# Weight-sum copies spread over the attention stage, the adding transfers begun after its middle, six of them tied to tiles of the out-projection's second half

## The chip, the cores and the metric

One core of one Trainium2 chip runs the whole program. The metric is device microseconds (us) of one launch, here the median of three runs. A core has a matmul engine (PE, with PEld for its weight loads), VectorE (DVE), ScalarE (ACT), GpSimd (POOL) and SyncE (SP). SP, ACT and POOL also issue DMAs; these run on 16 DMA engines that all issuers share. In the profile, q0 is the DMA queue that POOL feeds ("software_dynamic"), q1 the one that SP feeds and q10 the one that ACT feeds ("hardware_dynamic").

## The reference, cut to what matters

One encoder layer over 1024 tokens of width 1024, all float32. The projected tokens go to two groups of heads; both are concatenated, projected out and added to x; then comes an MLP with a squared ReLU.

```python
h = rms(x, norm1_g)
p = h @ w_in
mix_a = mlstm_group(...)             # 4 heads, chunkwise matrix memory, gated by sigmoid(o)
mix_b = diff_attention_group(...)    # 4 heads; two softmax maps each, subtracted; 128-query blocks
x = x + concat(mix_a, mix_b) @ w_out
u = square(relu(rms(x, norm2_g) @ w_ff1))
x = x + u @ w_ff2
```

## The kernel before

Every matmul of float32 data is made of three products of a high and a low part (`mm3`, and the same by hand in `product`, `coarse_step`, `fine_step`): an operand arrives "raw" by DMA, ACT writes its high part, and DVE or POOL subtracts that from the raw tile to get the low part.

The MLP's second product is done by two nested levels of a Strassen-Winograd scheme. It needs sums and differences of blocks of `w_ff2`. These are not made on an engine: a DMA copies one block to a scratch tensor in DRAM, and a second DMA adds another block to it in DRAM (`accum_op=add`). `s7`, `s6`, `s5` hold the sums of the coarse level (8 pieces of 512 KB each), `so[i, p]` those of the fine level (2 pieces each). In `coarse_sums` and `fine_sums`, "c7" is the copy into sum 7, "a7" the add to it, and so on. The copies of the first sums and all adds are issued by POOL: line 186 is the copy (`copy_in`), line 189 the add (`add_to`). They are first read some 90 us into the MLP or later.

Order of the work around the change. The attention stage runs from about 342 to 580 us. It is 32 items (a head and 128 queries each); their pieces, and those of other work, are pushed on a heap with a time in units of one item and are written out in order of that time, so that each engine gets its instructions in that order and then waits only for what its data need. In order of time:

- Item n: `att_logits` (PE `pl`, then DVE l.1442 with the bias `toe`), `att_exp` (ACT l.1448), `att_weights` (DVE l.1454 to l.1458), `att_across` (PE l.1465, ACT l.1469), `att_product` (PE `pav`, l.1477), ACT l.1482, a root on POOL (l.1486 and l.231) and DVE l.1491. Every fourth item loads the next head: `q` and `kk` by POOL (l.1412, l.1415), `toe` and `v` by SP (l.1418, l.1423).
- Times 0 to 12: the gate's units (`gate_unit`), which end in a write of `mx_dram` by POOL (l.1604).
- Time 15.2: `swap` gives the memory of the first stages to the out-projection's tiles and loads `mix` for its first half by POOL (`load_mix`, l.1515, four loads of 512 KB).
- Times 18.4 to 34: `first_half`, eight tiles of the out-projection for tokens 0 to 511. The raw weights of a tile come by SP (`split_ahead`, l.1552, tile `raw_wo`, two buffers); ACT makes the high part `hi_wo` (l.270, by the helper `act`), POOL the low part `lo_wo` (l.1559).
- From time 34.3: the second half, tokens 512 to 1023, eight tiles `n`: `h_part` (24 matmuls of 128x512), `h_room` (loads x), `h_add` (DVE l.1728), `h_square` (ACT l.1734, and a store of y on ACT's queue), `h_sum`. Here DVE makes `lo_wo`. Between them stand `row_norms(0)` (PE l.1522, DVE l.1524, POOL l.231, PE l.1529) and the first weights and inputs of the MLP (l.1798 and l.1801, loads at l.1817).

The copies and adds stand on the same heap with times of their own: the copies of "c7" from time -2.5 on, 0.8 apart, the last of the 16 copies at 12.2; the eight coarse adds from 5.6 to 13; the eight fine adds from 18 to 27. The order on the queue of POOL is thus that of these times. The later sums (c6 and a6, c3 and a3, c5 and a5) are issued in the MLP by another table, and are not touched.

Of the kernel before, what the change touches and what calls it, by code (L numbers as in the profile page):

```python
# [140 lines left out]
def hybrid_block_kernel(ctx: ExitStack, tc: tile.TileContext, xT, xR, w_v, w_k, w_c, w_va, w_qg, w_o, w_1, w_2, w_2q, vec, rel, outT):  # L141
    nc = tc.nc
# [27 lines left out]
    def w2_block(row, col):  # L170
        return w_2[2 * row + col]
# [19 lines left out]
    def chain(i, q):  # L191
        o = {p: so[i, p][q] for p in (5, 6, 7, 3)}
        x = {(rr, b): w2_fine(i, rr, b)[q] for rr in range(2) for b in range(2)}
        return {
            "c7": (copy_in, o[7], x[0, 0]), "c5": (copy_in, o[5], x[1, 1]), "a7": (add_to, o[7], x[1, 0]),
            "a5": (add_to, o[5], x[1, 0]), "c6": (copy_in, o[6], o[7]), "a6": (add_to, o[6], x[1, 1]),
            "c3": (copy_in, o[3], o[6]), "a3": (add_to, o[3], x[0, 1]),
        }

    def fine_sums(what, i):  # L200
        return [chain(i, q)[x] for x in what.split() for q in range(2)]

    def coarse_sums(what):
        return [{
            "c7": (copy_in, s7[j], w2_block(0, 0)[j]), "a7": (add_to, s7[j], w2_block(1, 0)[j]),
            "c6": (copy_in, s6[j], s7[j]), "a6": (add_to, s6[j], w2_block(1, 1)[j]),
            "c5": (copy_in, s5[j], w2_block(1, 0)[j]), "a5": (add_to, s5[j], w2_block(1, 1)[j]),
            "a3": (add_to, s6[j], w2_block(0, 1)[j]),
        }[what] for j in range(8)]

    def spread(first, each, transfers, put):
        for n, (f, *args) in enumerate(transfers):
            put((first + each * n, 10**6 + 100 + n, f, args))
# [10 lines left out]
    cst = const.tile([P, 32], F32, name="cst")  # L224
# [111 lines left out]
    with tc.tile_pool(reuse_waits="tile", name="ps0", bufs=1, space=PSUM) as ps0:  # L336
# [219 lines left out]
        for i in range(2):  # L556
            n, k = [f"n{2 * i}", f"n{2 * i + 1}"], [f"kr{2 * i}", f"kr{2 * i + 1}"]
# [109 lines left out]
        for i, slot in enumerate((0, 1, 2, 4)):  # L667
            y = i % 2
# [40 lines left out]
        for t in range(4):  # L709
            y = t % 2  # L710
# [59 lines left out]
    clock, table, made = [0.0], [], []  # L770

    def when(t, f, *args):
        heapq.heappush(table, (t + moved.get(len(made), 0.0), len(made), f, args))
        made.append(t)
# [744 lines left out]
    def row_norms(half):  # L1519
# [16 lines left out]
    A = dict(  # L1536
        G0=-0.05, G1=0.219, E0=0.984, E1=1.396, W=1.626, A0=2.667, A1=2.819, C0=2.714, C1=2.824, P=3.534, SQ=3.666,
        RS=3.676, ON=3.783, TU=4.131, TH=4.141, TL=4.177, LD=-2.901, LV=-1.095, PF=-4, PS=1.015, PE=0.388, PT=1.671,
        PB=1.957, PW=-3.566, PH=-2.613, PL=-1.973, PX=-0.258, SW=15.195, OF=18.423, OS=0.979, OE=0.323, OQ=0.587,
        OA=1.385, OW=-3.888, OH=-2.551, OL=-2.267, HF=34.3, HS=0.375, LM=33, HE=0.3, HQ=0.415, HA=0.425, HW=-1.4,  # L1540
        HH=-0.861, HL=-0.4, HX=-3.083, S2=35.3, N0=36.2, N1=36.9, XN=37.278, XD=0.78, XH=1.108, XL=1.118, WN=37.523,
        WD=0.8, WL=0.227, RE=35.494,
    )
    clock[0] = -99.0

    def split_ahead(tiles, src, lo_eng, t, pre, floor=-99.0):

        T = {}

        def room():  # L1550
            T[0] = tiles()
            nc.sync.dma_start(T[0][2][:, 0:1024], src)

        def hi():
            act(T[0][0][:, 0:1024], T[0][2][:, 0:1024], AF.Copy)

        def lo():
            h, l, raw = T[0]
            lo_eng.tensor_tensor(l[:, 0:1024], raw[:, 0:1024], h[:, 0:1024].bitcast(F32), op=ALU.subtract)

        floor = max(floor, A["SW"] + 0.01 if pre in "OH" else -99.0)
        when(max(t + A[pre + "W"], floor), room)
        when(max(t + A[pre + "H"], floor), hi)
        when(max(t + A[pre + "L"], floor), lo)
        return T

    def gate_pieces():

        w_at = [A["PF"] + 4 * h * A["PS"] for h in range(NH)]
        for h in range(NH):  # L1570
            T = gate_w[h] if h < 2 else split_ahead(lambda h=h: w_tiles(f"o{h}"), w_c[8 + h], nc.gpsimd, w_at[h], "P")
            for g in range(2):
                gate_unit(h, g, T, w_at[h] + 2 * g * A["PS"])
# [55 lines left out]
    def w_out(n, half=0):  # L1629
        raw = opool.tile([P, 1024], F32, tag="raw", name=f"raw_wo{half}{n}", bufs=2)  # L1630
        hi = opool.tile([P, 1024], F32R, tag="woh", name=f"hi_wo{half}{n}", bufs=3)
        return hi, opool.tile([P, 1024], F32R, tag="wol", name=f"lo_wo{half}{n}", bufs=3), raw
# [63 lines left out]
    def push(x):  # L1696
        heapq.heappush(table, x)

    def at_times(slots, transfers):
        for (f, *args), t in zip(transfers, slots):  # L1700
            push((t, 10**6 + 200 + len(table), f, args))

    spread(-2.5, 0.8, coarse_sums("c7") + fine_sums("c7 c5", 1), push)
    spread(9.2, 1.0, fine_sums("c7 c5", 2), push)
    at_times((5.6, 6.4, 7.5, 8.5, 10, 11, 12, 13), coarse_sums("a7"))
    at_times((18, 19, 20, 22, 23, 24, 26, 27), fine_sums("a7 a5", 1) + fine_sums("a7 a5", 2))
    gate_pieces()
    when(A["SW"], swap)
    first_half()
# [43 lines left out]
    def room_at(n):  # L1753
        return A["HF"] + u * ends[n - 3] + 0.01 if n > 2 else -99.0

    for n in range(KT):
        t = A["HF"] + u * parts_at[n][0][0]
        V = {"w": split_ahead(lambda n=n: w_out(n, 1), w_o[n], nc.vector, t, "H", room_at(n))}
        for p, first, end in parts_at[n]:
            when(A["HF"] + u * p, h_part, V, n, first, end)  # L1760
        t = A["HF"] + u * ends[n]
        when(max(t + A["HX"], A["S2"] + 0.02), h_room, n)
        when(t + A["HE"], h_add, V, n)
        when(t + A["HQ"], h_square, V, n)
        when(t + A["HA"], h_sum, V, n)

# [79 lines left out]
    for j in range(4):  # L1846
        t = A["XN"] + j * A["XD"]
# [3 lines left out]
        t = A["WN"] + j * A["WD"]  # L1851
# [19 lines left out]
    table = []  # L1871
# [36 lines left out]
    for c in range(N_FIRST):  # L1908
        when(max(2 * c - 1, 0), ops[1], c)
        ends_at[1, c] = max(2 * c, 1)  # L1910
        t = min(2 * c + 2, 2 * N_FIRST - 1)
        when(t, ops[2], c)
        ends_at[2, c] = t + 1
    t = 2 * N_FIRST
# [230 lines left out]
    step_at, t = [], T2  # L2145
# [230 lines left out]
                tt(o, o, banks[n][:, sl], op=add)  # L2376
                eng.dma_start(outT[n][:, HB + sl.start : HB + sl.stop], o)

    pace = cst[:, 25:26]

    def add_after(s, f, *args):
        nc.gpsimd.tensor_copy(pace, graw[s][:, 0, 0:1])
        f(*args)
# [5 lines left out]
    for s, (i, p, x) in enumerate(steps):  # L2389
        t, e = step_at[s], step_at[s + 1]  # L2390
# [29 lines left out]
        if not p and x == NJ - 1:  # L2420
            for n in range(4):
                f = t + 0.5 * (n + 1) + (-0.01 if i == 5 else 0.01)
# [12 lines left out]
    for k in range(2):  # L2435
# [5 lines left out]
        for m, (d, name, row, half) in enumerate(((r00, "ea", 0, 0), (r01, "eb", 0, 1), (zv, "ec", 1, 0), (zx, "ed", 1, 1))):  # L2441
            t = d0 + 1.2 + 1.6 * (2 * m + k)
# [95 lines left out]
```

## Time and profile before

| | before |
|---|---|
| three runs | 1233.06 us median (1230.11 to 1233.25) |
| the profiled execution, its own time | 1233.69 us |
| its span, first to last instruction | 1231.9 us |
| PE busy | 1212.0 us (98%) |
| PEld, DVE, ACT, POOL busy | 1035.4, 893.0, 693.3, 282.9 us |
| mean granted clock of PE | 0.996 |
| DMA | 290.47 MB, 236 GB/s over the span |
| POOL's adds in DRAM (l.189) | 32 of coarse, 24 of fine sums, each issue about 0.81 us on POOL |

The profiled execution's span lies 1.8 us under its own time; that time is 0.6 us over the median. PE is busy nearly all the time, so what it loses stands in a few idle gaps. A profile line of a wait reads: who waited, on what, for how long, how often, and the longest one. In the timeline, the bracket is the idle time of that engine just before the instruction and what ended it. A row of a window has the busy time of PE, PEld, DVE, ACT and POOL with counts, then the granted clock, the mean busy share of the 16 DMA engines and what they moved in GB/s.

### The profile page before, as it was taken

How to read it: one execution, taken by the hardware profiler on the slowest of the kernel's cores; microseconds unless marked ns; L12 is line 12 of the kernel's file. 1: busy time of each engine (PE TensorE's matmuls, PEld its weight loads, DVE VectorE, ACT ScalarE, POOL GpSimd, SP SyncE). 2: the span in 40 equal slices, each digit the busy share in tenths (PEclk: the TensorE clock that was granted, in tenths of full speed). 3: DMA queues.
4: the chain of work that ended last, by engine and by line, in shares of the span. 5: the costliest groups of instructions: out<-in, count | busy, mean ns of one | idle time of the engine just before them, and what ended most of it. 6: DMA issues, size and time to landing. Idle time of an engine off the chain costs nothing.

```text
span 1231.9 us, 18385 instructions
## 1 busy us (share of the span) xinstructions
PE 1212.0 (98%) x6781; PEld 1035.4 (84%) x6781; DVE 893.0 (72%) x1253; ACT 693.3 (56%) x1200; POOL 282.9 (23%) x339
## 2 busy tenths in 40 slices
PE   9999999999999979999999999999999999999998
PEld 7889888888878868888887878888888999989987
DVE  7885568983267776765879886666657878888865
ACT  7785457676356666564455544545446556465532
POOL 2135323652356655431000000010100000010100
PEclk9999999999999989999999999999999999999999
DMA  9972665344589998745544789999899889998977
GB/s 283 229 248 104 208 145 132 99 139 129 162 305 279 289 303 225 208 138 205 179 165 144 265 280 306 259 256 276 255 275 355 281 287 337 353 306 249 257 260 260
DMA packets 115406, 290.47 MB, mean 236 GB/s; under 512 B 11632, under 2 KB 24432, under 8 KB 114544
## 3 DMA queue, kind: packets, MB, share of 16 engines
q1 hardware_dynamic: 85076, 202.88, 48.2%
q0 software_dynamic: 18432, 65.05, 22.7%
q10 hardware_dynamic: 11808, 21.37, 4.7%
q8 instruction: 53, 0.87, 0.3%
q14 instruction: 37, 0.30, 0.1%
HBM read 229.91 MB, written 112.82 MB: 278 GB/s over the span
## 4 chain that ended last, share of the span: by engine, by line
PE 80%; DMA 9%; DVE 4%; ACT 3%; issue 2%; POOL 1%; SPq 0%; ACTq 0%; DVEq 0%; POOLq 0%
PE m L1885 6%; PE m L1887 6%; PE m L1886 6%; PE z L2269 5%; PE z L2268 5%; PE z L2267 5%; PE pav L1477 5%; PE pl L1437 4%; PE pva L1347 4%; PE z L2288 3%; PE z L2287 3%; PE z L2286 3%; PE pw L280 3%; PE pw L282 2%; PE pw L281 2%; PE pa L1465 2%
## 5 line engine op out<-in xcount | busy, mean ns | idle before, releaser
L1442 DVE CUSTOM_DVE_ANT_0 l<-pl,toe 128x1024 f32<-128x1024 f32 x64 | 76.3, 1221 | 15.9 <-PE pl L1437 14.4
L189 POOL DMA_DIRECT2D so<-in_w_2q_dram x24 | 20.2, 842 | 277.2 <-DMA so<-so 242.0
L1934 ACT ACTIVATE sq<-sq 128x512 f32<-128x512 f32 x48 | 30.3, 630 | 83.3 <-DVE sq L1973 65.0
L1448 ACT ACTIVATE l<-l,sm 128x1024 f32<-128x1024 f32 x64 | 73.1, 1148 | 0.5 <-DVE sm L1442 0.5
L1477 PEld LDWEIGHTS pav<-v,at 128*128 128x128 f32 x512 | 63.0, 195 | 3.4 <-issue 1.1
L1477 PE MATMUL pav<-v,at 128*128 128x128 f32 x512 | 64.1, 279 | 0.0
L189 POOL DMA_DIRECT2D s<-in_w_dram x32 | 26.7, 844 | 157.0 <-DMA s<-in_w_dram 94.6
L1437 PE MATMUL pl<-kk,q 64*128 64x512 f32 x384 | 56.0, 415 | 3.0 <-DVE sm L1442 3.0
L2269 PE MATMUL z<-weh,wa0l 128*128 128x512 f32 x144 | 56.3, 391 | 0.1
L2267 PE MATMUL z<-weh,wa0h 128*128 128x512 f32 x144 | 56.2, 390 | 0.0
L2268 PE MATMUL z<-wel,wa0h 128*128 128x512 f32 x144 | 56.2, 390 | 0.0
L280 PE MATMUL pj_c<-hhi,w_c 128*128 128x512 f32 x128 | 53.4, 417 | 0.0
L280 PE MATMUL pw<-mix,hi_wo 128*128 128x512 f32 x128 | 52.0, 406 | 0.0
L282 PE MATMUL pj_c<-hhi,w_c 128*128 128x512 f32 x128 | 50.2, 392 | 0.0
L282 PE MATMUL pw<-mix,lo_wo 128*128 128x512 f32 x128 | 50.0, 391 | 0.0
L281 PE MATMUL pj_c<-hlo,w_c 128*128 128x512 f32 x128 | 50.0, 390 | 0.0
L281 PE MATMUL pw<-mix,hi_wo 128*128 128x512 f32 x128 | 49.9, 390 | 0.0
L2288 PE MATMUL z<-zgh,zwl 128*128 128x256 f32 x168 | 47.6, 284 | 0.8 <-DVE zwl L1801 0.8
L1437 PEld LDWEIGHTS pl<-kk,q 64*128 64x128 f32 x384 | 35.1, 186 | 15.6 <-DVE sm L1442 4.6
L2286 PE MATMUL z<-zgh,zwh 128*128 128x256 f32 x168 | 47.6, 283 | 0.3 <-ACT zwh L1798 0.3
L2287 PE MATMUL z<-zgl,zwh 128*128 128x256 f32 x168 | 47.5, 283 | 0.0
L1458 DVE SCALAR_TENSOR_TENSOR l<-l,sm,l 128x1024 f32<-128x1024 f32 x32 | 42.8, 1337 | 1.1
(544 smaller groups left out, 4061.6 us busy)
## 6 DMA issues: line engine op xcount, KB each, us to landing
s<-in_w_dram POOLq DMA_DIRECT2D x40, 512.0 KB, 8.3
so<-in_w_2q_dram POOLq DMA_DIRECT2D x32, 512.0 KB, 8.5
g_dram<-gs SPq DMA_DIRECT2D x64, 256.0 KB, 5.8
zw<-s SPq DMA_DIRECT2D x32, 512.0 KB, 7.2
g<-g_dram SPq DMA_DIRECT2D x32, 512.0 KB, 8.6
wide<-g_dram SPq DMA_DIRECT2D x24, 512.0 KB, 8.5
zw<-so SPq DMA_DIRECT2D x24, 512.0 KB, 3.5
g_dram<-sq ACTq DMA_DIRECT2D x42, 256.0 KB, 4.2
```

The costliest lines, as they stand in the source:

```text
L280: nc.tensor.matmul(out, ahi, bhi, start=start, stop=False)
L281: nc.tensor.matmul(out, ahi, blo, start=False, stop=False)
L282: latest[0] = nc.tensor.matmul(out, alo, bhi, start=False, stop=stop).ins
L1437: nc.tensor.matmul(it.pl[x][:, sl], hd.q[r, i, qi * P : (qi + 1) * P], hd.kk[r, j, sl], start=n == 0, stop=n == 2)
L1442: nc.vector.tensor_tensor_reduce(lt, it.pl[m], hd.toe[:, off : off + S], 1.0, 3.0e38, ALU.add, ALU.min, it.sm[:, m : m + 1])
L1477: nc.tensor.matmul(it.pav[:, 0:P], at, it.head.v[:, c], start=c == 0, stop=c == NC - 1)
L2267: nc.tensor.matmul(p, wh, gh, start=go, stop=False, skip_group_check=True)
L2268: nc.tensor.matmul(p, wh, gl, start=False, stop=False, skip_group_check=True)
L2269: nc.tensor.matmul(p, wl, gh, start=False, stop=end, skip_group_check=True)
L2286: nc.tensor.matmul(o, wh[:, j, nn], gh[:, j], start=go, stop=False, skip_group_check=True)
L2287: nc.tensor.matmul(o, wh[:, j, nn], gl[:, j], start=False, stop=False, skip_group_check=True)
L2288: nc.tensor.matmul(o, wl[:, j, nn], gh[:, j], start=False, stop=end, skip_group_check=True)
```

## The change

The 16 first copies get a list of times of their own, from -2.5 to 21.2, where they had stood at -2.5 to 12.2: twelve of them up to 13.2, four at 18.2 to 21.2. The 16 first adds are taken as one list. Ten of them (the eight coarse ones, and the two that add to `so[1, 7]`) stand at 19.7 to 29.6, 1.1 apart. The other six are pushed right behind `h_add` of the tiles n = 1 to 6 of the second half, each by `add_with`: a copy of one column of that tile's sum to the scratch column `pace` on POOL, which has to wait for the tile, and then the add. `pace` is the column that `add_after` uses later for other adds; its definition only moves up. No transfer is added or taken away; six copies of 128x1 on POOL are new.

```diff
-    spread(-2.5, 0.8, coarse_sums("c7") + fine_sums("c7 c5", 1), push)
-    spread(9.2, 1.0, fine_sums("c7 c5", 2), push)
-    at_times((5.6, 6.4, 7.5, 8.5, 10, 11, 12, 13), coarse_sums("a7"))
-    at_times((18, 19, 20, 22, 23, 24, 26, 27), fine_sums("a7 a5", 1) + fine_sums("a7 a5", 2))
+    first_copies = coarse_sums("c7") + fine_sums("c7 c5", 1) + fine_sums("c7 c5", 2)
+    first_adds = coarse_sums("a7") + fine_sums("a7 a5", 1) + fine_sums("a7 a5", 2)
+    at_times((-2.5, -1.7, -0.9, -0.1, 1.2, 2.6, 4.2, 6.2, 7.6, 9.2, 11.2, 13.2, 18.2, 19.2, 20.2, 21.2), first_copies)
+    spread(19.7, 1.1, first_adds[:10], push)
+    pace = cst[:, 25:26]
+
+    def add_with(n, f, *args):
+        nc.gpsimd.tensor_copy(pace, y[1][n][:, 0:1])
+        f(*args)
+
     gate_pieces()
...
         when(t + A["HE"], h_add, V, n)
+        if 1 <= n < 7:
+            f, *args = first_adds[9 + n]
+            push((t + A["HE"] + 0.005, 10**6 + 200 + len(table), add_with, (n, f, *args)))
         when(t + A["HQ"], h_square, V, n)
```

The order of PE, ACT, DVE and SP stays as it was; only POOL's changes. Around `swap`, POOL had this before (s and so are the scratch tensors; `128x1024` marks an add, `16x8192` a copy; mx_dram, q, kk and mix as above; sm are the roots of the items):

```order
L189 DMA s_6_183<-in_w_dram 128x1024
L186 DMA so_1_210<-in_w_2q_dram 16x8192
L1456 TENSOR_SCALAR sm_4266<-sm_4266 128x1
L1486 TENSOR_TENSOR sm_4113<-sm_4113 128x1
L231 TENSOR_TENSOR sm_4113<-sm_4113,mhalf 128x1
L189 DMA s_7_184<-in_w_dram 128x1024
L1412 DMA q_4405<-q_dram_76 128x1024
L1415 DMA kk_4407<-k_dram_67 128x2x512
```

and has this now; the adds are gone, and one copy stands behind the loads of kk:

```order
L186 DMA so_0_201<-in_w_2q_dram 16x8192
L1456 TENSOR_SCALAR sm_4186<-sm_4186 128x1
L1486 TENSOR_TENSOR sm_4039<-sm_4039 128x1
L231 TENSOR_TENSOR sm_4039<-sm_4039,mhalf 128x1
L1456 TENSOR_SCALAR sm_4257<-sm_4257 128x1
L1486 TENSOR_TENSOR sm_4106<-sm_4106 128x1
L231 TENSOR_TENSOR sm_4106<-sm_4106,mhalf 128x1
L1412 DMA q_4392<-q_dram_76 128x1024
L1415 DMA kk_4394<-k_dram_67 128x2x512
L1415 DMA kk_4394<-k_dram_68 128x2x512
L186 DMA so_1_202<-in_w_2q_dram 16x8192
```

In the second half, POOL had after the items' last root only the two roots of the row norms (rc), and behind them adds of the MLP:

```order
L231 TENSOR_TENSOR sm_5707<-sm_5707,mhalf 128x1
L231 TENSOR_TENSOR rc_6064<-rc_6064,mhalf 128x4
L231 TENSOR_TENSOR rc_6322<-rc_6322,mhalf 128x4
L189 DMA so_0_203<-in_w_2q_dram 128x1024
L189 DMA so_1_204<-in_w_2q_dram 128x1024
```

and now has the six copies (of the tile y) and adds, one pair ahead of the first rc, five between the two:

```order
L231 TENSOR_TENSOR sm_5701<-sm_5701,mhalf 128x1
L1710 COPY cst<-y_0_5963 128x1
L189 DMA so_0_201<-in_w_2q_dram 128x1024
L231 TENSOR_TENSOR rc_6060<-rc_6060,mhalf 128x4
L1710 COPY cst<-y_1_5964 128x1
L189 DMA so_1_202<-in_w_2q_dram 128x1024
L1710 COPY cst<-y_1_5964 128x1
L189 DMA so_0_213<-in_w_2q_dram 128x1024
```

The four pairs that follow these in the list, up to the second rc, read alike.

More of the change, by code (lines that the diff above doesn't have):

```diff
@@ L2377, in finish @@
                 eng.dma_start(outT[n][:, HB + sl.start : HB + sl.stop], o)
-    pace = cst[:, 25:26]
     def add_after(s, f, *args):
```

## The prediction

> **What bounds the kernel now.** The page first. PE is busy for 98% of the span, so a change pays only where PE stands idle or cold. I then cut the span into stretches; in these columns (stretch, length, busy PE, PEld, DVE, ACT, POOL, clock, DMA share, GB/s) one place in the attention stage stands out:
>
> ```profile
> PE 1212.0 (98%) x6781; PEld 1035.4 (84%) x6781; DVE 893.0 (72%) x1253; ACT 693.3 (56%) x1200; POOL 282.9 (23%) x339
> 430.00:440.00 10.00, 9.36 (x73) 7.69 (x73) 9.57 (x17) 7.77 (x17) 6.21 (x13) 1.00 1.07 309
> 440.00:450.00 10.00, 8.51 (x63) 6.74 (x62) 6.16 (x11) 3.67 (x9) 1.69 (x2) 1.00 1.09 402
> 450.00:460.00 10.00, 5.62 (x34) 5.31 (x36) 6.63 (x11) 7.24 (x16) 7.33 (x9) 0.66 0.65 194
> 460.00:480.00 20.00, 20.00 (x135) 16.71 (x132) 14.47 (x26) 12.44 (x24) 10.30 (x13) 1.00 0.91 234
> ```
>
> From 430 to 460 PE loses 6.5 us, at a DMA share of 1.07 and 1.09, and the clock then falls to 0.66; from 460 on PE is full. Next the waits of 428 to 462, and the chain through it:
>
> ```profile
> ACT hi_wo L270 <- DMA raw_wo<-in_w_o_dram: 6.0, 1, 6.0
> 435.18 14.46 DMA raw_wo<-in_w_o_dram
> 450.63 1.24 ACT l L1448 x2
> ```
>
> The raw weights of the out-projection's first tile need 14.46 us. ACT stands at their high part, with two items' exponentials behind it, and for those wait DVE (l.1458) and, by the last bracket below, PE. The timeline gives the sizes:
>
> ```profile
> 449.67 1.06 ACT L270 ACTIVATE hi_wo<-raw_wo 128x1024 fp32r<-128x1024 f32 x1 [5.98 <-DMA raw_wo<-in_w_o_dram]
> 441.60 1.97 PE L1437 MATMUL pl<-kk,q 64*128 64x512 f32 x12
> 446.35 2.18 PE L1437 MATMUL pl<-kk,q 64*128 64x512 f32 x12
> 454.38 1.09 PE L1465 MATMUL pa<-ident,l 128*128 128x128 f32 x4 [5.85 <-DVE l L1458]
> 455.26 3.33 PE L1477 MATMUL pav<-v,at 128*128 128x128 f32 x16
> 458.95 1.66 PE L1437 MATMUL pl<-kk,q 64*128 64x512 f32 x12
> ```
>
> ACT was free at 443.69 (449.67 - 5.98). Two items' `pl` follow each other after 4.75 us (441.60 to 446.35); the next comes after 12.60. So the place costs 7.85 us: 5.85 of idling, the rest in matmuls run cold after it.
>
> Why was the tile late? The queues of 426 to 438 and then of 438 to 450 (the row of packets is the latter's), and landing times of `v` over the attention and of `raw_wo` at 460 to 535:
>
> ```profile
> q0 software_dynamic: 1007, 3.43, 103.1%
> q1 hardware_dynamic: 10, 0.03, 0.7%
> q<-q_dram POOLq DMA_DIRECT2D x1, 512.0 KB, 9.9
> DMA packets 2231, 4.79 MB, mean 399 GB/s; under 512 B 140, under 2 KB 1164, under 8 KB 2231
> q1 hardware_dynamic: 1490, 2.23, 52.7%
> q0 software_dynamic: 741, 2.56, 56.5%
> DMA to landing us min/median/max: 3.8/4.0/8.1
> DMA to landing us min/median/max: 3.4/5.0/6.5
> ```
>
> Until 438 POOL's queue alone fills all engines and works off a backlog (`q` lands after 9.9 us). SP's queue, which has `v` in small packets and then the tile, gets nearly nothing until then and about half afterwards.
>
> **The change, part by part.** *Price of a transfer.* Two adds nearly alone on q0 (520.2 to 534.5), then two copies with one store of mx_dram (362.5 to 372):
>
> ```profile
> so<-in_w_2q_dram POOLq DMA_DIRECT2D x2, 512.0 KB, 7.3
> q0 software_dynamic: 288, 1.05, 41.5%
> q0 software_dynamic: 214, 1.57, 42.6%
> ```
>
> 41.5% of 14.3 us is 5.9: some 3.0 us of all 16 engines per add. 42.6% of 9.5 is 4.05 for three: 1.35 per copy or store.
>
> *Adds and copies leave the time before the tile.* POOL's copies and adds of 512 KB in the last 32 us before it lie between the first two of these rows:
>
> ```profile
> 404.91 0.54 POOL L186 DMA_DIRECT2D so<-in_w_2q_dram  x1
> ...
> 427.04 0.86 POOL L189 DMA_DIRECT2D s<-in_w_dram  x1
> 434.76 0.37 SPq L1423 DMA_DIRECT2D v<-va_dram  x1
> 436.48 2.23 POOL L1515 DMA_DIRECT2D mix<-mx_dram  x4
> ```
>
> With three more adds and three more copies between them these are four adds and four copies, 4 x 3.0 + 4 x 1.35 = 17.4 us of engine time. The new order keeps three copies (times 9.2, 11.2, 13.2), 4.1 us. 13.3 us of transfer go from a stretch whose backlog was about 6 (9.9 for `q`, against 3.8 for `v` when nothing is ahead). The backlog should be gone by 427; what stays in front is q, kk, one copy and mx_dram.
>
> When does the tile land then? Its issue at 435.18 stays, since SP's order does. Early end: `v` 3.8 after 434.76, the tile 3.4 later, 442.0, before ACT comes at 443.69: no wait. Late end: all of v, two raw tiles, mx_dram and the four loads of mix, 8 x 0.524 = 4.19 MB, at 399 GB/s from 436.48, so 447.0: a wait of 3.3. I take 1.4, a little under the middle, because the tile is in front of half of these bytes. ACT still does the 1.06 of the high part within one item; between 0 and 1.06 of it reaches PE, I take 0.4. Gain: 7.85 - 1.4 - 0.4 = 6.05.
>
> The Trainium skill speaks against this: "DMA: Bandwidth & Descriptors", section "Queues, rings and completion order", says that a DMA engine takes turns between the queues that have work, a packet each. By that a backlog on POOL's queue costs SP's half of the engines, never all; the trace's 52.7% beside 56.5% agrees, and the 0.7% before 438 would be mostly SP having asked for nothing until 434.76. By this rule the gain would be the 2.55 of the first rival below, by the rows on the backlog 6.05.
>
> *The start of the attention* (to 404): one copy fewer between 342 and 351, adds gone. PE has no gap there that a DMA ends, so 0.
>
> *The middle, 455 to 530.* Before, three adds stood at times 18 to 20; now four copies and two adds stand at 18.2 to 21.2: 4 x 1.35 - 3.0 = 2.4 us more in about 24, on a share of 0.91. That fills the engines, but loads run far ahead:
>
> ```profile
> 466.48 0.37 SPq L1552 DMA_DIRECT2D raw_wo<-in_w_o_dram  x1
> 489.51 2.45 POOL L1559 TENSOR_TENSOR lo_wo<-raw_wo,hi_wo 128x1024 fp32r<-128x1024 f32 x1
> ```
>
> That is the fourth tile, loaded 23 us ahead of its low part; a landing of even 14.46 is hidden. 0. POOL's issues (0.54 to 0.9) move between the same kind of roots: 0. Without that cover each late tile would cost what the first did.
>
> *Six adds behind tiles 1 to 6 of the second half.* On POOL: six copies, which the same copy elsewhere (l.2382) prices at 0.2 to 1.1 us, and six issues of 0.8 to 0.9. The queue behind a waiting copy holds only the other pairs and the two rc roots; POOL idles 11.83 us ahead of the first of these, so the one pair in front fits: 0.
>
> ```profile
> L2382 POOL COPY cst<-g x8: 184/742/1118, 1093.1 to 1163.0; 128x1 f32<-128x1 f32 x8
> 591.91 1.40 POOL L231 TENSOR_TENSOR rc<-rc,mhalf 128x4 f32<-128x4 f32 x1 [11.83 <-DVE rc L1524]
> ```
>
> On the DMA engines: five of the adds, 15 us, go into 590 to 622, where 0.45 x 10 + 0.44 x 10 + 0.59 x 12 = 16 are taken:
>
> ```profile
> 590.00:600.00 10.00, 10.00 (x53) 8.53 (x52) 6.90 (x11) 3.64 (x6) 1.40 (x1) 1.00 0.45 164
> 600.00:610.00 10.00, 10.00 (x45) 8.27 (x45) 9.94 (x14) 6.20 (x8) 0.00 (x0) 1.00 0.44 152
> 610.00:622.00 12.00, 12.00 (x54) 9.95 (x53) 8.72 (x11) 4.40 (x6) 0.00 (x0) 1.00 0.59 188
> 602.26 0.38 SPq L1552 DMA_DIRECT2D raw_wo<-in_w_o_dram  x1
> 606.71 1.06 ACT L270 ACTIVATE hi_wo<-raw_wo 128x1024 fp32r<-128x1024 f32 x1 [0.96 <-DMA raw_wo<-in_w_o_dram]
> 609.70 1.22 DVE L1559 TENSOR_TENSOR lo_wo<-raw_wo,hi_wo 128x1024 fp32r<-128x1024 f32 x1
> 619.97 0.69 DVE L1728 TENSOR_TENSOR y<-pw,y 128x512 f32<-128x512 f32 x1 [2.52 <-PE pw L282]
> ```
>
> 31 of 32: just full. The last tile is the tightest. It lands by 606.7; high and low part take 1.06 + 1.22; PE ends it at 619.97, and its 24 matmuls (10 us per 45) take 5.4, so PE needs it at 614.5. Slack 5.5. In the middle, where adds were about all the time, such a tile landed after 6.5 at worst, 3.4 at best; 3.1 later is hidden. Lower bound 0 (the adds free nothing here); upper bound a landing of 14.46 instead of 4.4, 10.1 later, 4.6 lost. I take 0.4, near the row of the same kind of traffic.
>
> Sum: 6.05 - 0.4 = 5.65 us less. On the profiled execution's 1233.69 that is 1228.0; it lies 0.6 above the median, and on the median of 1233.06 it gives 1227.4.
>
> **The rivals.** *The tile stays late, 1230.5.* If not the backlog but sharing with the loads of mix holds it, only the start of SP's service moves, by at most 3 us (438 to 435). For it: after 438 SP's queue had its half, and more than half of the packets were small ones that take turns with mix's. Against it: with the backlog gone, `v` is through before mix begins. The tile then moves by 1 to 3; with 1.5 the wait stays at 4.5 and the gain is 7.85 - 4.5 - 0.4 - 0.4 = 2.55.
>
> *The second half takes it back, 1234.6.* The adds hold SP's tiles as the backlog did. The place is the last tile; it decides from a landing of 9.9 us on (4.4 + 5.5), and net from 6.05 us of loss. At 14.46 PE loses 4.6 there; the weights of the MLP's first products come behind it on the same queue, equally late, against a gap of 2.52 on DVE: 10.1 - 2.52 = 7.6 in all. 1233.06 - 6.05 + 7.6 = 1234.6. Against it: an add comes once per tile of 5.4 us and needs 3.0, where before 438 adds, copies and the attention's loads came together.
>
> **How the numbers follow.** A change under about 0.3%, 3.7 us, cannot be told from none. My forecast (1225 to 1229) has 0.70; the late tile 0.16 (0.13 within 0.3%); the second half 0.08 (0.05 within); the rest, all idle and cold time gone or something unseen, 0.06. Faster 0.77, same 0.18, slower 0.05. The low end is the whole 7.85 off the median, 1225.2, and 1.2 for where a median of three can lie among runs 3 us apart; the high end takes in the late tile and 1 us of the same.
>
> **What would show it.** Right: `hi_wo`'s wait of 5.98 under 3, `q` before it landing in about 5, `pl` no more than 8 us apart there, the clock of that stretch near 1, PE full at 584 to 622. Wrong: the wait over 4, or a new row of PE waiting for `hi_wo` or `lo_wo` in the second half.

## The result, and the profile after

| | before | after |
|---|---|---|
| median of the runs timed side by side | 1234.47 us (1230.11 to 1237.09) | 1226.59 us (1223.67 to 1231.93) |
| the profiled execution, its own time | 1233.69 us | 1227.73 us |
| its span | 1231.9 us | 1225.9 us |

The ratio of the times is 0.9939, with a 95% interval of 0.9925 to 0.9953: faster by 5.8 to 9.3 us, 7.88 between the medians of thirteen runs each. The two profiled executions, one of these runs each, differ by 5.96 us. The changed kernel's lines from l.1700 on stand 6 to 9 lower (`h_add` is l.1734, its copy to `pace` l.1710).

First the same stretches as before, in the same columns (stretch, length, PE, PEld, DVE, ACT, POOL, clock, DMA share, GB/s):

```profile
430.00:440.00 10.00, 9.36 (x74) 7.73 (x73) 9.57 (x17) 7.73 (x17) 6.17 (x13) 1.00 0.99 310
440.00:450.00 10.00, 9.81 (x76) 8.09 (x75) 8.41 (x18) 9.60 (x20) 6.69 (x8) 1.00 1.07 403
450.00:460.00 10.00, 9.77 (x69) 7.99 (x69) 8.09 (x16) 5.43 (x13) 6.84 (x11) 1.00 0.81 238
```

From 440 to 460 PE is busy for 19.58 of 20 us, where it was 14.13, and the clock stays at 1.00. From 440 to 450 the DMA engines are as full as they were (1.07 against 1.09); what the change relieved lies ahead of that. The timeline of the changed kernel at the place of the stall:

```profile
441.63 1.96 PE L1437 MATMUL pl<-kk,q 64*128 64x512 f32 x12
443.62 1.05 ACT L270 ACTIVATE hi_wo<-raw_wo 128x1024 fp32r<-128x1024 f32 x1
446.37 2.20 PE L1437 MATMUL pl<-kk,q 64*128 64x512 f32 x12
451.50 0.49 PE L1437 MATMUL pl<-kk,q 64*128 64x512 f32 x1
452.21 1.65 PE L1437 MATMUL pl<-kk,q 64*128 64x512 f32 x11 [0.23 <-DVE sm L1442]
453.79 0.50 PE L280 MATMUL pw<-mix,hi_wo 128*128 128x512 f32 x1
```

`hi_wo` has no bracket any more: the tile was there when ACT came. The two items' `pl` start at the same times as before (441.6 and 446.4), the third after 5.13 us instead of 12.60. The first matmul of the out-projection stands here at 453.79; before, it was this row:

```profile
460.55 0.50 PE L280 MATMUL pw<-mix,hi_wo 128*128 128x512 f32 x1
```

The queues of 426 to 438 in the changed kernel:

```profile
q0 software_dynamic: 874, 2.62, 71.3%
q1 hardware_dynamic: 476, 0.24, 7.0%
...
q<-q_dram POOLq DMA_DIRECT2D x1, 512.0 KB, 3.9
```

POOL's queue has 71.3% instead of 103.1%, SP's comes in before 438, and `q` lands after 3.9 us instead of 9.9. In the second half, where the six adds now are, the windows:

```profile
590.00:600.00 10.00, 10.00 (x46) 8.28 (x45) 9.86 (x14) 4.11 (x5) 3.36 (x3) 1.00 0.91 225
600.00:610.00 10.00, 10.00 (x46) 8.29 (x45) 8.29 (x10) 5.38 (x6) 4.07 (x4) 1.00 0.84 216
610.00:622.00 12.00, 12.00 (x63) 10.16 (x62) 7.81 (x12) 3.41 (x5) 4.34 (x3) 1.00 0.91 239
```

And from the timeline the last tile's load and its high part:

```profile
595.53 0.38 SPq L1552 DMA_DIRECT2D raw_wo<-in_w_o_dram  x1
602.93 1.06 ACT L270 ACTIVATE hi_wo<-raw_wo 128x1024 fp32r<-128x1024 f32 x1 [3.92 <-DMA raw_wo<-in_w_o_dram]
```

The engines' share, 0.44 to 0.59 before, is 0.84 to 0.91, the tile lands after 7.4 us instead of 4.4, ACT waits 3.92, and PE has no gap: the wait is hidden.

### The profile page after: what moved, and what is told of

Read it like the earlier page. It is cut to its first block, busy times and chain, and to the rows that moved or that the text cites. A ratio compares the mean times of both kernels' runs of the same rounds, so it can differ in the third digit from the quotient of the medians.

```text
span 1225.9 us, 18401 instructions
## 1 busy us (share of the span) xinstructions
PE 1211.5 (99%) x6781; PEld 1034.3 (84%) x6781; DVE 892.4 (73%) x1253; ACT 693.8 (57%) x1200; POOL 289.6 (24%) x345
## 4 chain that ended last, share of the span: by engine, by line
PE 83%; DVE 5%; DMA 5%; ACT 2%; issue 2%; POOL 1%; SPq 0%; ACTq 0%; DVEq 0%; POOLq 0%
PE m L1894 6%; PE m L1896 6%; PE m L1895 6%; PE z L2278 5%; PE z L2277 5%; PE z L2276 5%; PE pav L1477 4%; PE pva L1347 4%; PE pl L1437 3%; PE z L2297 3%; PE z L2296 3%; PE z L2295 3%; PE pvz L486 3%; PE pw L280 3%; PE pw L282 2%; PE pw L281 2%
## 5 line engine op out<-in xcount | busy, mean ns | idle before, releaser
L1347 PE MATMUL pva<-w_va,hhi 128*128 128x512 f32 x128 | 43.5, 403 | 0.0
```

Of the source, the lines that this page charges most:

```text
L1347: latest[0] = nc.tensor.matmul(p[:, j * HB : (j + 1) * HB], a, b, start=k == 0 and i == 0, stop=k == KT - 1 and i == 2).ins
```

## The experiments

Theory one, that of the prediction: the adds' backlog on POOL's queue held the first tile; what counts is how many us of transfers stand ahead of it. Its rival there: the tile shares the engines with the loads of `mix`, whatever stands ahead. Each run below was timed beside the kernel before (medians there 1233.1 to 1234.5); "wait" is ACT's idle time before the first tile's `hi_wo` in the one profiled execution. A difference between two rows whose intervals overlap is not shown.

| run | median, us | ratio to before, 95% | wait, us |
|---|---|---|---|
| the changed kernel | 1226.59 | 0.9925 to 0.9953 | 0 |
| adds moved, copies not | 1227.78 | 0.9940 to 0.9970 | 0 |
| copies moved, adds not | 1233.34 | 0.9984 to 1.0015 | 6.00 |
| two adds moved (12 and 13) | 1227.14 | 0.9938 to 0.9973 | 0 |
| two adds moved (10 and 11) | 1231.19 | 0.9964 to 0.9992 | 0.41 |
| `mix` later, backlog kept | 1228.15 | 0.9948 to 0.9975 | 0 |
| tile ahead of `v` | 1227.07 | 0.9923 to 0.9957 | 0 |
| `v` in large packets | 1229.12 | 0.9936 to 0.9968 | 0.89 |
| changed, one add put back | 1234.20 | 0.9993 to 1.0016 | 6.20 |
| the same, a copy cut | 1235.07 | 0.9994 to 1.0020 | 6.26 |
| changed, six adds in an idle stretch | 1227.73 | 0.9917 to 0.9955 | 0 |
| changed, twelve adds behind tiles | 1229.78 | 0.9949 to 0.9977 | 0 |
| changed, no first adds | 1225.37 | 0.9922 to 0.9948 | 0 |

**Adds alone, copies alone.** The changed kernel with the copies at their old times, and the kernel before with the copies at their new ones:

```diff
-    at_times((-2.5, -1.7, ..., 20.2, 21.2), first_copies)
+    spread(-2.5, 0.8, coarse_sums("c7") + fine_sums("c7 c5", 1), push)
+    spread(9.2, 1.0, fine_sums("c7 c5", 2), push)
```

> The adds stand as in the changed kernel (ten from time 19.7 on, six behind tiles), the copies as before (0.8 apart from -2.5, then four up to 12.2). Theory one, the adds' backlog held the first tile: the last 32 us before the tile keep four copies, 5.4 us of engine time, against 4.1 in the changed kernel and 17.4 before, so the tile comes in time here too: no wait of ACT for raw_wo over 0.5 us, q before it lands in about 4 to 5 us, time 6.5 to 8 us under the kernel before, as the changed kernel. Rival, that the copies' new places carry half of the gain or more: 4 us under before or less, with a wait of 2 us or more left.

```diff
-    spread(-2.5, 0.8, coarse_sums("c7") + fine_sums("c7 c5", 1), push)
-    spread(9.2, 1.0, fine_sums("c7 c5", 2), push)
+    first_copies = coarse_sums("c7") + fine_sums("c7 c5", 1) + fine_sums("c7 c5", 2)
+    at_times((-2.5, -1.7, ..., 20.2, 21.2), first_copies)
```

> The copies stand as in the changed kernel, the adds as before (eight coarse ones at 5.6 to 13, eight fine ones at 18 to 27). Theory one: four adds and three copies are left before the tile, 16.1 us of engine time against 17.4 before, so the backlog of about 6 falls by 1.35: q lands after about 8.5 us, ACT's wait is 4.6 instead of 6.0, time 1 to 1.5 us under before, which is no difference that can be told. Rival, the copies carry half or more: 3.5 us or more under before.

The adds do it; the spread of the copies does nothing that can be told. Without the wait the first run is 5.3 us under before (3.7 to 7.4), a little less than the 6.5 to 8 expected. But in the second run the wait was to fall to 4.6 with the backlog, and it did not. Its timeline:

```profile
447.10 1.06 ACT L270 ACTIVATE hi_wo<-raw_wo 128x1024 fp32r<-128x1024 f32 x1 [6.00 <-DMA raw_wo<-in_w_o_dram]
451.81 1.08 PE L1465 MATMUL pa<-ident,l 128*128 128x128 f32 x4 [5.87 <-DVE l L1458]
```

The wait is 6.00 against 5.98 of before, PE's idling 5.87 against 5.85. It does not shrink in proportion to what stands ahead; that was the first sign that the theory had the wrong measure.

**Two adds moved.** Two of the four adds that stand in the last 32 us before the tile:

```diff
-    at_times((5.6, 6.4, 7.5, 8.5, 10, 11, 12, 13), coarse_sums("a7"))
+    at_times((5.6, 6.4, 7.5, 8.5, 10, 11, 28, 29), coarse_sums("a7"))
```

> The kernel before, with only the last two coarse adds moved from times 12 and 13 to 28 and 29; two adds and four copies stay in the 32 us ahead of the tile. If the backlog was about 6 us of engine time, as q's landing of 9.9 against 3.8 says, then two adds of 3.0 are just all of it: q lands in 4 to 5, ACT's wait falls under 1.5, time 5 to 7.5 us under before. If the backlog is only what happens to be above water, and the whole 13.3 us have to go: half of the wait stays (3 us), and the time is 3 to 4 us under before.

As expected in the first case: no wait, and with two of the sixteen adds a gain that cannot be told from that of the whole change. Removing 1.35 us gave nothing, removing 6.0 gave it: an edge seemed to lie between.

**`mix` later.** The kernel before, where only the issue of the four loads of `mix` moves, from 436.5 to 442.5 us:

```diff
     when(A["SW"], swap)
+    push((A["SW"] + 0.9, 10**6 + 200 + len(table), fetch_mix, (0,)))
...
-        load_mix(0)
+        open_mix(0)
```

> The kernel before, with the four loads of mix issued some 7 us later (time 16.1 instead of 15.2, about 444 us instead of 436.5) and nothing else moved; the backlog of adds and copies up to 438 stays. If the tile was late because of the backlog alone, that is, if v and the tile simply start late, they still start at 438 and need 1.6 MB at 399 GB/s: 442 to 443, so that the wait would be gone here as well, 6 to 7.5 us under before, unless mix itself is then late for the out-projection, which is first needed at about 454. That would show that the backlog and the loads of mix hold the tile together, neither of them alone. If SP's queue is held by something else than these two (its own packets, the tile's issue), the wait stays over 4 and the time within 2 us of before.

The wait is gone with every add and copy in its old place:

```profile
442.49 2.23 POOL L1518 DMA_DIRECT2D mix<-mx_dram  x4
442.26 1.06 ACT L270 ACTIVATE hi_wo<-raw_wo 128x1024 fp32r<-128x1024 f32 x1
```

So backlog and `mix` hold the tile together. (The time is 4.9 us under before, less than the 6 to 7.5 expected: PE still idles 1.24 us there for DVE's l.1458, and the out-projection's first matmul comes 1.4 later after the items' `pl` than in the other runs without a wait.) That falls between theory one and its rival, and called for another.

**Theory two.** The loads of `v` (packets of 512 bytes, 128 x 8 = 1024 of them) stand just ahead of the tile on SP's queue. Suppose that each engine takes turns between SP's queue and POOL's, a packet each. One that still has packets of `v` when the data of `mix` come (4096 bytes a packet) then passes one small packet for each large one, and the tile behind `v` waits until `mix` is nearly through. The count of packets can show it. In these rows the packets of 512 bytes are those under 2 KB less those under 512 B, and all of them are `v`'s. Before, 438 to 442 and 442 to 450:

```profile
DMA packets 1229, 1.56 MB, mean 390 GB/s; under 512 B 40, under 2 KB 925, under 8 KB 1229
DMA packets 1002, 3.23 MB, mean 404 GB/s; under 512 B 100, under 2 KB 239, under 8 KB 1002
```

885 of the 1024 are through by 442, and 139 straggle through the next 8 us. The changed kernel, 436 to 440 and 440 to 448, with the queues of each:

```profile
DMA packets 1204, 1.10 MB, mean 275 GB/s; under 512 B 39, under 2 KB 1063, under 8 KB 1204
q1 hardware_dynamic: 1138, 0.90, 73.0%
q0 software_dynamic: 66, 0.20, 15.3%
DMA packets 822, 3.23 MB, mean 404 GB/s; under 512 B 76, under 2 KB 76, under 8 KB 822
q0 software_dynamic: 519, 1.92, 65.1%
```

All 1024 are through by 440, while q0 has 66 packets in 4 us; `mix` comes after that (519). Copies alone, 438 to 446 (its `v` was issued at 432.18): 238 - 85 = 153 are still to come at 438.

```profile
DMA packets 975, 3.25 MB, mean 407 GB/s; under 512 B 85, under 2 KB 238, under 8 KB 975
```

The next two runs take away `v`'s place and `v`'s small packets, with backlog and `mix` as before.

**The tile ahead of `v`.** For the head of item 16 alone:

```diff
-            when(n + A["LV"] if n else -97.0, att_load_v, it)
+            when(n + (A["LV"] if n != 16 else -0.7) if n else -97.0, att_load_v, it)
```

> The kernel before, with the load of v for the head of item 16 moved on SP's queue from just ahead of the first tile to just behind it; backlog and loads of mix unchanged. Theory two, formed after the first four runs (an engine that still has backlog gives v's 512-byte packets one turn for each 4096-byte packet of mix, and the tile stands behind v on SP's queue): the tile no longer stands behind small packets, takes equal turns with mix from the backlog's end at 438 to 440 on, and lands by 444; ACT's wait is under 1, time 5 to 7.5 us under before. If bytes alone decide (tile, v and mix share what the engines move, the backlog first): the place in SP's queue gains 0.5 MB of 4, 1.3 us, the wait is 4 to 5 and the time 1 to 2 us under before.

The stall is gone and the gain is that of the whole change, but not for the reason expected. SP's timeline:

```profile
419.18 0.43 SPq L1552 DMA_DIRECT2D raw_wo<-in_w_o_dram  x1
434.14 0.37 SPq L1423 DMA_DIRECT2D v<-va_dram  x1
```

The tile is issued at 419.18, not 435.18. Its memory must have been free 15 us earlier than it was used; SP stood at the issue of `v` (which by the code has two buffers, both in use until then) with the tile behind it. SP's waits of before, 400 to 440, show it:

```profile
SPq L1423 <- PE pav L1477: 14.9, 1, 14.9
```

So this run does not test the packets. It shows a second condition of the stall, which the prediction took as given (its issue "stays, since SP's order does"): a waiting instruction on SP's queue.

**`v` in large packets.** The stores now write the small packets, at 282 to 329 us:

```diff
-    va_dram = tc.dram_tile([NC, P, 512], F32, name="va_dram")
+    va_dram = tc.dram_tile([NH, P, NC, P], F32, name="va_dram")
...
-        nc.scalar.dma_start(va_dram[t], vt)
+        nc.scalar.dma_start(va_dram[:, :, t].rearrange("h p v -> p h v"), vt.rearrange("p (h v) -> p h v", v=P))
...
-        nc.sync.dma_start(hd.v, va_dram[:, :, h * P : (h + 1) * P].rearrange("c p v -> p c v"))
+        nc.sync.dma_start(hd.v, va_dram[h])
```

> The kernel before, with va_dram laid out by heads, so that v is loaded in packets of 4096 bytes instead of 512 (its eight stores at 282 to 329 us then write 512 bytes a packet instead of 2048). Order, bytes, backlog and mix unchanged. Theory two (small packets take turns with mix's large ones): v and the tile together are 16 large packets per engine against 32 of mix and end 5 to 6 us after the backlog, at 443 to 446; ACT's wait is 0 to 2.5, time 4.5 to 7.5 us under before, unless the small stores cost something at 282 to 340. If the size of packets plays no part (bytes alone, or SP's queue waiting for POOL's): wait 5 to 6, time within 1 us of before.

```profile
444.01 1.06 ACT L270 ACTIVATE hi_wo<-raw_wo 128x1024 fp32r<-128x1024 f32 x1 [0.89 <-DMA raw_wo<-in_w_o_dram]
```

Same bytes, same order, same backlog, same `mix`: the wait falls from 5.98 to 0.89, within the 0 to 2.5 expected. With that edit alone the late tile is gone but for 0.89: the size of `v`'s packets is what turned a shared engine into a late tile.

**Where two adds or one may stand.** The other two of the four adds moved; and, in the changed kernel, one add put back just ahead of the loads of `q` and `kk`:

```diff
-    at_times((5.6, 6.4, 7.5, 8.5, 10, 11, 12, 13), coarse_sums("a7"))
+    at_times((5.6, 6.4, 7.5, 8.5, 28, 29, 12, 13), coarse_sums("a7"))
```

> The kernel before, with the coarse adds of times 10 and 11 moved to 28 and 29; those of 12 and 13 (423 and 427 us) stay. The same count as in the run that moved 12 and 13, 11.4 us of transfers in the 32 us ahead of the tile, but later. If the amount decides: no wait, 5 to 7 us under before, as there. If it decides whether POOL's queue is drained, and v's small packets are through, before the loads of mix start (theory two): the two late adds and q, kk behind them keep the queue busy up to about 436, as in the run with the copies alone moved, where the wait was still 6.0; so a wait of 3 to 6 and 0 to 4 us under before.

```diff
-    spread(19.7, 1.1, first_adds[:10], push)
+    spread(19.7, 1.1, first_adds[1:10], push)
+    at_times((13.05,), first_adds[:1])
```

> The changed kernel, with one of its ten spread adds put back to time 13.05, just ahead of the loads of q and kk (about 427 us); three copies and this add, 7.1 us of transfers, stand in the 32 us ahead of the tile. If the amount decides (11.4 gave no wait): no wait, 6.5 to 8 us under before. By theory two this one add moves the end of POOL's queue by up to 3.0, from 436 to about 438, into the time when mix starts: v's last small packets then take turns with mix, a wait of 2 to 5, and the time is 1 to 5 us under before.

One add gives the whole gain back: ratio 0.9993 to 1.0016. There was no backlog for it to add to: from 426 to 429 the DMA engines moved nothing.

```profile
DMA packets 16, 0.00 MB, mean 0 GB/s; under 512 B 16, under 2 KB 16, under 8 KB 16
```

Still the tile is late:

```profile
450.37 1.06 ACT L270 ACTIVATE hi_wo<-raw_wo 128x1024 fp32r<-128x1024 f32 x1 [6.20 <-DMA raw_wo<-in_w_o_dram]
```

Its packets at 438 to 442 and 442 to 450, and then those of the run with the two late adds:

```profile
DMA packets 1254, 1.52 MB, mean 381 GB/s; under 512 B 39, under 2 KB 1008, under 8 KB 1253
DMA packets 928, 3.25 MB, mean 407 GB/s; under 512 B 96, under 2 KB 151, under 8 KB 928
```

```profile
DMA packets 1341, 1.56 MB, mean 390 GB/s; under 512 B 44, under 2 KB 1068, under 8 KB 1341
DMA packets 876, 3.25 MB, mean 406 GB/s; under 512 B 97, under 2 KB 97, under 8 KB 876
```

With one add back, 55 of `v`'s 1024 packets straggle, and the tile is as late as with 139 or 153; by theory two I had expected a wait of 2 to 5, not 6.20. With the two late adds none does, and the wait is 0.41, where by theory two I had expected 3 to 6: I had not foreseen well enough when POOL's queue would be drained. That kernel stands on the edge: of its twelve timings five lie at 1226.4 to 1228.9 and seven at 1231.0 to 1236.1, and the profiled one is of the first group. 7.1 us of transfers ahead of the tile can thus cost all of it, and 11.4 nothing; the amount is refuted as the measure. What the runs have in common is whether `v` is through on every engine when the data of `mix` begin: by the trace's packet records that holds, to 0.6 us, in every run with the small packets and the tile behind them that has no wait.

The same records show why the wait does not grow with what is left. With one add back, packets of `v` start one by one, about every 0.19 us, from 442.0 to 448.2, and the last 20 follow 0.02 apart. Its rows of 443 to 448 and 448 to 449 have 29 packets in five us, then 21 in one:

```profile
DMA packets 545, 2.05 MB, mean 409 GB/s; under 512 B 54, under 2 KB 83, under 8 KB 545
DMA packets 132, 0.40 MB, mean 399 GB/s; under 512 B 23, under 2 KB 44, under 8 KB 132
```

A packet of `mix` takes 0.17 us. One engine passes one small packet for each large one, until its share of `mix` is through; an estimate from these figures: 4 x 128 / 16 = 32 packets, 32 x 0.19 = 6.1 us. The waits of the four late runs are 5.98 to 6.26, whether 55 packets are left or 153.

**A copy cut into small packets.** 55 is near one engine's share of `v`, 1024 / 16 = 64: one engine seems to be late. In the last run the copy behind `kk`, 16 packets of 32768 bytes, became 128 of 4096:

```diff
+    _, dst, src = first_copies[11]
+    first_copies[11] = (lambda d, s: nc.gpsimd.dma_start(d, s, max_dma_last_dim=4096)), dst, src
```

> The run with one add put back, with one more edit: the copy that stands behind the loads of kk there (about 430 us) is cut into packets of 4096 bytes, 128 of them, instead of 16 of 32768. Place, bytes and everything else unchanged. If one DMA engine that is late with its 32768-byte packet is what holds the tile (it begins with v when mix is already there, and v's packets on it then take one turn in two): the packets spread, v is through on all engines by 442 as in the run with two late adds, the wait is 0 to 2 and the time 4.5 to 7.5 us under before. If the time at which POOL's queue is drained decides, whatever its packets: wait 4 to 6.5, time within 1.5 us of before.

Nothing changes: a wait of 6.26, and 154 - 94 = 60 stragglers at 440 to 448.

```profile
DMA packets 909, 3.24 MB, mean 405 GB/s; under 512 B 94, under 2 KB 154, under 8 KB 909
```

The long packets are not what makes an engine late. The packet records show one that was late before the copy, at `kk`. With one add back, fifteen of the copy's sixteen packets start by 436.6 and the last at 439.32; until then single packets of `kk` (2048 bytes) still start, and one of them takes 0.93 us against a median of 0.10. With the copy cut, one of `kk` takes 1.17. Why, and which engine it is, stays open; the records do not number the engines. The Trainium skill, "DMA: Bandwidth & Descriptors", section "Latency and other measured facts", says that two of the sixteen engines are usually slower and suspects the descriptors of GpSimd's queue. Leftovers near one engine's share, or two, would fit; no run here shows it.

**The second half.** The six adds at 30.5 to 34 instead of behind tiles; and two behind each tile instead of one:

```diff
+    at_times((30.5, 31.2, 31.9, 32.6, 33.3, 34.0), first_adds[10:])
...
-        if 1 <= n < 7:
-            f, *args = first_adds[9 + n]
-            push((t + A["HE"] + 0.005, 10**6 + 200 + len(table), add_with, (n, f, *args)))
```

> The changed kernel, with the six adds that stand behind tiles moved into the stretch before the second half where the DMA engines idle (times 30.5 to 34, some 535 to 560 us). The first tile as in the changed kernel: no wait. If the six adds behind tiles cost nothing there, as the trace after says: the time is that of the changed kernel, 6.5 to 8 us under before, with the last tile of the second half landing in 4 to 5 us instead of 7.3. If the 0.7 us that the changed kernel loses at 663 to 728 came from them: 7 to 8.5 under, the best so far. If pacing behind tiles is needed (the adds meet the loads of mix for the second half there): a wait at 550 to 590 and 3 us or more lost.

```diff
-    spread(19.7, 1.1, first_adds[:10], push)
+    spread(19.7, 1.1, first_adds[:4], push)
...
-            f, *args = first_adds[9 + n]
-            push((t + A["HE"] + 0.005, 10**6 + 200 + len(table), add_with, (n, f, *args)))
+            for f, *args in first_adds[2 + 2 * n : 4 + 2 * n]:
+                push((t + A["HE"] + 0.005, 10**6 + 200 + len(table), add_with, (n, f, *args)))
```

> The changed kernel, with two adds behind each of the tiles 1 to 6 of the second half instead of one (twelve there, four of the sixteen at 19.7 to 23): 6.0 us of engine time per tile of 5.4, beside 0.45 of the engines taken by loads and stores, so that the engines are asked for more than they can give from about 585 to 625. By turns (theory two: raw tiles have packets of 4096 bytes, as the adds have, and so get half of the engines whenever they ask): the last tile lands in 8 to 10 us, at the edge of its slack (9.9), PE loses 0 to 1.5 us, the time is 5 to 7.5 us under before. By the rival of the prediction (POOL's backlog holds SP's tiles as the first tile was held, 14.5 us): PE loses 4.6 us or more at the last tile and more at the weights behind it, the time is 0 to 3 us under before.

In the idle stretch the adds make no difference that can be told (0.9917 to 0.9955 against 0.9925 to 0.9953). Twelve behind tiles reach PE:

```profile
592.81 0.45 SPq L1552 DMA_DIRECT2D raw_wo<-in_w_o_dram  x1
604.85 1.06 ACT L270 ACTIVATE hi_wo<-raw_wo 128x1024 fp32r<-128x1024 f32 x1 [8.45 <-DMA raw_wo<-in_w_o_dram]
605.96 0.50 PE L280 MATMUL pw<-mix,hi_wo 128*128 128x512 f32 x1 [0.92 <-ACT hi_wo L270]
607.22 0.50 PE L282 MATMUL pw<-mix,lo_wo 128*128 128x512 f32 x1 [0.53 <-DVE lo_wo L1559]
...
616.64 1.02 PE L1522 MATMUL pr<-ones,yacc 128*128 128x1 f32 x8 [1.42 <-DVE yacc L1745]
```

The last tile lands after 12.0 us, and PE loses 0.92 + 0.53 + 1.42 = 2.9. That lies between the two cases expected, a landing of 8 to 10 with 0 to 1.5 lost and one of 14.5 with 4.6 lost. The ratios, 0.9963 against 0.9939, differ by 0.0024 or 3.0 us; their intervals just overlap, so the time alone does not show the loss.

**No first adds.** The changed kernel without them; the sums then lack their second block.

```diff
-    spread(19.7, 1.1, first_adds[:10], push)
...
-        if 1 <= n < 7:
-            f, *args = first_adds[9 + n]
-            push((t + A["HE"] + 0.005, 10**6 + 200 + len(table), add_with, (n, f, *args)))
```

> The changed kernel without the sixteen first adds; the sums they complete lack their second block. It bounds what these adds still cost where they now stand. If they cost nothing there (all of PE's waits they cause are gone): the time of the changed kernel, 6.5 to 8 us under before. If they still cost something, by traffic in the middle, in the second half or at the start of the MLP (the 0.7 us at 663 to 728): 8.5 us or more under before, and the gaps of PE at 685 and 728 go.

0.9922 to 0.9948 against 0.9925 to 0.9953: where the adds now stand they cost nothing that can be told. The changed kernel has taken what was to be had from them.

## Why the prediction came out right, step by step

- *The time.* 1227.4 was forecast, 1226.59 measured. The gain was forecast at 5.65 us; the medians differ by 7.88, and 5.65 lies just under the interval of 5.8 to 9.3. The median before, 1233.06 of three runs, is 1234.47 of thirteen; from that one the forecast would have been 1228.8, still in the range but 2.2 off. That the time came within 0.8 is luck. The steps below explain the 6.0 of the two profiled executions; the rest of the 7.88 no trace shows. One execution varies by more than that where nothing differs: in the changed kernel, in the one with six adds in an idle stretch, and in those with twelve adds behind tiles and with none, POOL's order up to 437 is the same, and the way from the attention's first gap of PE (343.92 in the changed kernel) to the `pl` at 436.75 takes 92.8, 94.0, 91.3 and 91.3 us, at a clock of 0.90, 0.80, 1.00 and 1.00 in 343 to 360.
- *The bound and the place.* Held: PE gained where the chain of waits had shown it, and nowhere else.
- *The ends of the range.* As worked out they are 1225.2 - 1.2 = 1224.0 and 1230.5 + 1 = 1231.5, wider than the 1225 to 1229 that was given 0.70. The measured time lies in both.
- *7.85 us at the place.* Held as its ceiling: the third `pl` came 7.47 earlier (12.60 - 5.13).
- *A wait of 1.4 left ("I take 1.4").* It measured 0. "with the backlog gone, `v` is through before mix begins", said there against the first rival, is what happened (1024 of 1024 packets by 440), so the tile stood in front of all of mix, not of half. Too cautious by 1.4.
- *0.4 for ACT's high part.* The third `pl` is 7.85 - 7.47 = 0.38 late, the size taken, though no run shows that ACT's high part is the reason. But from there to the first matmul of the out-projection another 0.7 goes (6.76 earlier, not 7.47): `pl` waits for DVE at 452.21 and is spread over 2.4 us instead of 1.7. Not in the sum.
- *The start and the middle, 0.* Held; PE has no new gap at 345 to 430 or 460 to 590.
- *The six adds, 0.4, the last tile 3.1 later.* It landed 3.0 later (7.4 against 4.4) and cost nothing. `y` of the last tile is stored 6.74 earlier, as much as the first half had gained.
- *0.7 us lost in the MLP, not in the sum.* The rows of one matmul pair, of before and of after:

```profile
667.35 0.50 PE L1886 MATMUL m<-x4l,wd0h 128*128 128x512 f32 x1 [0.40 <-DVE x4l L1801]
733.76 0.47 PE L1885 MATMUL m<-x3h,wbh 128*128 128x512 f32 x1 [0.76 <-DVE w L1968]
```

```profile
660.64 0.50 PE L1895 MATMUL m<-x4l,wd0h 128*128 128x512 f32 x1 [0.44 <-DVE x4l L1810]
727.75 0.47 PE L1894 MATMUL m<-x3h,wbh 128*128 128x512 f32 x1 [0.72 <-DVE w L1977]
```

  The stretch took 66.4 and 67.1 us. In the profiled executions of all kernels here it takes 65.2 to 67.9, 67.1 without the first adds and 66.7 with the adds alone moved; so the 0.7 is within what one execution varies, and is not shown to come from the change.
- *The sum.* 7.85 - 0.4 - 0.7 - 0.7 = 6.0, as the spans of the two profiled executions show (1231.9 to 1225.9), against 5.65: the term too cautious by 1.4 and the 0.4 not lost were made up by two of 0.7 that were missing. That the forecast comes so near these 6.0 is luck. At the place itself the change gains 6.8: from the `pl` at 436.7 to the out-projection's first matmul it is 23.85 us before and 17.04 after, and within 0.02 of that in six other runs without a wait.
- *The reason given was half of it.* "13.3 us of transfer go from a stretch whose backlog was about 6" treats the stall as a quantity. The runs show an edge: the tile needs `v` through before the data of mix, and 55 late packets of 1024 cost as much as 139. The gain came since after the change `v` is through 1 us before those data (439.9 against 440.9 in the packet records); one add put back crosses the edge.
- *The first rival.* Its mechanism, sharing with the small packets and `mix`, is real: it is what made the stall 6 us long, and the run with large packets and the run with `mix` later show it. Its forecast of 2.55 us failed because after the change `v` never shares with `mix`. The rule that the prediction weighed, that a DMA engine takes turns between its queues a packet each (the Trainium skill, "DMA: Bandwidth & Descriptors", section "Queues, rings and completion order"), agrees with the stragglers. Here the turns go by the packets that the profile counts: one of 512 bytes, one of 4096, every 0.19 us. So it did not speak against the change; it was the reason why clearing the queue in time paid in full.
- *The second rival.* It "decides from a landing of 9.9 us". At 12.0, with twelve adds, PE lost 2.9, at 7.4 nothing: the point lies between, as placed, and the change stays 2.5 us under it.

## What to carry to other kernels

A load that is late behind a full queue need not be late in proportion: ask what is in front of it on its own queue, in what packets, and what begins on the other queues before that is through. Here two of sixteen adds moved, the loads of `mix` six us later, or the tile ahead of a waiting `v` each took the wait away, with 4.9 to 7.1 us gained between medians, and one add put back in the wrong place brought it back. Before spreading many transfers, look for the one order of two instructions that makes the edge, and time a kernel that stands on it more than once.

## What the runs showed of the hardware that I had not expected

- 55 of 1024 packets, passed singly as by one DMA engine, hold a tile of 512 KB for 6.2 us, while the mean over the engines looks no different (407 GB/s at 442 to 450 with the stall, 406 without).
- The data of `mix` come 4.4 us after its issue in the changed kernel (issued from 436.52, first packet at 440.91), and q0 has only 66 packets at 436 to 440. `v` got through in that pause. Issued at 442.49 instead, they came after 2.2 us; what sets the delay is not shown.
- `v` in packets of 512 bytes takes about 4 us with the engines to itself (1024 packets at 436 to 440), and cutting a copy's 32768-byte packets to 4096 changed nothing.
